# Queries and keys of the last 1024 tokens: seven quadrant products instead of eight

## The chip, the cores and the metric

The kernel runs on one core of a Trainium2 chip. The core's engines work in parallel, each through its own instruction list in order: PE multiplies matrices, ACT, DVE and POOL work on tiles element by element, SP (like the others) issues transfers. Engines wait for each other through semaphores. The metric is the time of one execution in microseconds (us); less is better.

## The reference

One layer of a decoder trunk on 2048 tokens of width 1024, all in float32. Only its first product matters here:

```
hn = _rmsnorm(h, ln_mix[i])
z = hn @ w_in[i]                       # (2048, 1024) @ (1024, 2048)
q = z[..., :512] * (HEAD_DIM ** -0.5)
k = z[..., 512:1024]
v = z[..., 1024:1536]
u = z[..., 1536:]
att = _dilated_attention(q, k, v, slopes)
pool = _multiscale_pool(u, pool_w[i], pool_scale[i])
h = h + concatenate([att, pool]) @ w_out[i]
```

`_multiscale_pool` takes trailing means of u over 2, 4, 8 and 16 tokens (one window for each group of 128 channels), subtracts the token, and multiplies by a 128x128 matrix for each group. A gated MLP, a gate on per-layer embeddings and a last norm follow; the change does not touch them.

## The kernel before, in words

A float32 product is done as three matmuls (`mm3`, L88): each operand is split into a rounded high part (a cast on ACT) and the low rest (a subtraction on DVE or POOL; `split`, L83), and high times high, high times low and low times high are added in PSUM.

`phase_project` (L170) computes z from chunks of tokens that go through it one after the other: chunk 0 (tokens 0 to 255), chunk 1 (256 to 511), chunks 2, 3 and 4 (512 tokens each). Each chunk has four groups of 512 output channels: 0 = q, 1 = k, 2 = v, 3 = u. The list in `order` gives 0, 1, 2, 3, and 0, 1, 3, 2 for chunk 4. A group sums over eight blocks of 128 inputs. One block is one **step**: four tiles by three matmuls of 128x512. A group so has eight steps, and fills four of the eight banks of PSUM; six banks go round in turn among the groups, one ("st") takes the sums of squares and the spread norm, one ("py") the small product of the pooling.

The split weights of q, k and v stay resident from chunk 0. Those of u are loaded in each chunk: `ahead` (L270) issues the loads and, three steps before the use, the ACT cast `wh` and the POOL low `wl`; there are three buffers of each.

The order in which each engine gets its instructions is the order in which the code calls them, and the engines keep to it (`manual_schedule`). Work beside the matmuls is spread by hand:

- After each step `tk.tick()` runs what `tk.later(n, ...)` put off by n steps.
- Step by step in group k, `square` puts the next chunk's squares into `acc` (ACT square, DVE add; one buffer `sq`). In group v `scale` and `spread_` make the norm: small PE products, POOL's power `pw`, four DVE instructions and two PE products into bank "st". In group u `norm_a` multiplies the next chunk's tokens by the norm on DVE, `norm_b` casts the high part (ACT) and subtracts for the low part (DVE).
- A finished group is taken from its banks: q and k by ACT and DVE and stored by SP, v into `vt`, whose stores go out on SP, and for chunk 4 on POOL's queue.
- `pool_branch` (L410) takes u from PSUM on ACT, and for each of its four channel groups later sums the windows on DVE (`ws`; 1, 2, 3 and 4 additions), subtracts the token, splits (ACT `dh`, DVE `dl`), multiplies into "py" (PE), and takes that out (ACT `mh`, DVE `ml`, two stores on POOL's queue). `ml` in `ACFG` says how many steps after the group each starts: 1, 3, 5, 11, and 1, 3, 5, 7 for chunk 4. This work falls into the next chunk's q and k groups, and for chunk 4 into its v group.

Of the kernel before, what the change touches and what calls it, by code (L numbers as in the profile page):

```python
# [168 lines left out]

def phase_project(tc, g, xT, w_in, pool_w, rcnt):  # L170
# [4 lines left out]
    with ExitStack() as ctx:  # L175
        wres = ctx.enter_context(tc.tile_pool(name="a_w", bufs=1, reuse_waits="tile"))
        sb = ctx.enter_context(tc.tile_pool(name="a_sb", bufs=1, reuse_waits="tile"))
        psum = ctx.enter_context(tc.tile_pool(name="a_ps", bufs=6, space=PSUM, reuse_waits="tile"))
# [24 lines left out]
        def load_w(pool, raw, grp, k, tag, bufs, low=None):  # L203
            hi = pool.tile([P, 512], F32R, tag=tag + "h", bufs=bufs, name=f"wh{grp}_{k}")
# [37 lines left out]
        def norm_a(st, k):  # L242
            xk = st.xs[k][:, : st.n]
            nc.vector.tensor_tensor(xk, xk, st.inv[:, : st.n], op=ALU.mult)

        def norm_b(st, k):
            hi = sb.tile([P, CH], F32R, tag="hnh", bufs=KD, name=f"hnh{k}")
            lo = sb.tile([P, CH], F32R, tag="hnl", bufs=KD, name=f"hnl{k}")
            n = st.n
            st.hn.append((hi[:, :n], lo[:, :n]))  # L250
            gain = g.vec[:, V_MIX + k : V_MIX + k + 1]
            nc.scalar.activation(hi[:, :n], st.xs[k][:, :n], AF.Copy, scale=gain)  # L252
            st.low = lambda: nc.vector.scalar_tensor_tensor(  # L253
                lo[:, :n], st.xs[k][:, :n], gain, fp(hi[:, :n]), op0=ALU.mult, op1=ALU.subtract
            )
# [15 lines left out]
        def ahead(i):  # L271
            while done[0] < len(wants) and wants[done[0]][0] <= i:
                w, c, grp, k = wants[done[0]]
                done[0] += 1
                fetch_to(w)
                low = ACFG["low"][min(c, 2)][grp][k % 2]
                low = nc.vector if low else nc.gpsimd
                raw = raws.pop((c, grp, k))
                if grp < 3:
                    held[grp, k] = load_w(wres, raw, grp, k, f"w{grp}", KD, low)  # L280
                else:
                    held[grp, k] = load_w(sb, raw, grp, k, "wu", 3, low)
            fetch_to(i + ACFG["ld"] if i < 8 * 3 - ACFG["ld"] - ACFG["la"] - 1 else i + ACFG["lu"])

# [6 lines left out]
        step = 0  # L291
        for c, (t0, n) in enumerate(chunks):
            cs = slice(t0, t0 + n)
            final = c == len(chunks) - 1
            nxt = None
            for gi, grp in enumerate((0, 1, 2, 3) if not final else (0, 1, 3, 2)):
                if gi == 2 and not final:
# [3 lines left out]
                ps = [psum.tile([P, CH], F32, tag="b1", name=f"z{c}_{grp}_{j}") for j in range(nt)]  # L301
                apart = final and grp == 2
                for k in range(KD if not apart else 0):
# [3 lines left out]
                    ahead(step + ACFG["la"])  # L307
                    step += 1
# [9 lines left out]
                    if gi == 0 and k == 6 and not final:  # L318
# [3 lines left out]
                    if gi == 3 and not final:  # L322
# [15 lines left out]
                    if gi == 0 and c > 0 and k < 2:  # L338
# [57 lines left out]
            cur = nxt  # L396
# [13 lines left out]
def pool_branch(nc, g, sb, psum, c, q, ps, t0, n, tail, rc, pw_h, pw_l, zpair, final):  # L410
# [57 lines left out]
    g.ticker.later(ACFG["ml"][1 if final else 0][q], means)  # L468
# [1432 lines left out]
def tile_layer(ctx, tc, xT, pT, vec, w_in, pool_w, w_out, w_up, w_down, w_gate, w_ple, near_b, far_b, rcnt, outT, upto=9):  # L1901
# [39 lines left out]
    g.dd = [{p: dr.tile([P, CH], F32, tag=f"dd{q}{p}", name=f"dd{q}{p}") for p in ("t1", "t2", "t3", "t4")} for q in range(NF // 2)]  # L1941
    g.h1 = per(KD, [P, S], F32, "h1")
# [85 lines left out]
```

## Time and profile before

| | us |
|---|---|
| median of 3 runs (lowest, highest) | 2395.49 (2394.4, 2397.76) |
| the profiled execution's own time | 2395.75 |
| its span in the profile | 2394.0 |
| PE busy in the span | 2320.2 (97%) |
| DVE, ACT, POOL busy | 1714.3, 1123.5, 571.1 |
| share of PE in the chain that ended last | 78% |

"Busy" is the time an engine spends in instructions. A row of a timeline reads: start (us from the span's start), busy us, engine, line, operation, out<-in by the program's names, shape, and in brackets the idle time ahead of it with the instruction that ended it. A row with x3 is three neighbouring instructions of one kind. A row by groups reads: busy us in all, mean ns of one | idle us ahead of them, and what ended it. `PEclk` is the clock that PE was granted, 1.00 being full speed; over the span its mean is 0.987. In the trace, chunk 2's u group and the start of chunk 3 lie around 194 to 240 us, and the last v group of `phase_project` at about 398 us.

### The profile page before, as it was taken

To read this page: it belongs to the slowest core of one execution; us is meant where nothing else is said; L and a number is where in the kernel's file an instruction comes from. 1 tells how busy PE (TensorE), PEld (TensorE's weight loads), DVE (VectorE), ACT (ScalarE), POOL (GpSimd) and SP (SyncE) were. 2 spreads that over 40 slices of the span, in tenths; PEclk is the share of its full clock that TensorE was granted. 3 is DMA by queue.
4 is the path that set the end of the run, shared out by engine and by line. 5 is a ranking of instruction groups with operands and counts; after the bars stand their busy time and mean duration, and the time that the engine had idled before them with its cause. 6 is when DMAs were issued, how large, how long until landed. Compare 5 with 4: busy or idle time off the path is not lost.

```text
span 2394.0 us, 32736 instructions
## 1 busy us (share of the span) xinstructions
PE 2320.2 (97%) x11251; PEld 1962.7 (82%) x11251; DVE 1714.3 (72%) x2684; ACT 1123.5 (47%) x2040; POOL 571.1 (24%) x552
## 2 busy tenths in 40 slices
PE   8999999999989989999999999999999999999998
PEld 7888887988868868888887787888878888888888
DVE  6645445888864668999999998777766565755665
ACT  5332234988832245454447353544444444444332
POOL 3322122356620133344430664000020000001000
PEclk9999999999999999999999999999999999999999
DMA  7534436877576664556567787444487776754332
GB/s 232 185 132 164 179 130 248 269 239 241 161 262 216 214 203 144 189 189 207 189 212 246 265 277 248 156 147 146 141 317 254 240 243 204 224 172 154 119 102 93
DMA packets 240550, 475.99 MB, mean 199 GB/s; under 512 B 37472, under 2 KB 63904, under 8 KB 237312
## 3 DMA queue, kind: packets, MB, share of 16 engines
q1 hardware_dynamic: 205040, 394.64, 50.2%
q0 software_dynamic: 15696, 51.49, 6.0%
q10 hardware_dynamic: 19648, 27.77, 3.3%
q8 instruction: 88, 1.44, 0.3%
q14 instruction: 78, 0.64, 0.1%
HBM read 309.14 MB, written 156.79 MB: 195 GB/s over the span
## 4 chain that ended last, share of the span: by engine, by line
PE 78%; DVE 8%; DMA 5%; issue 3%; ACT 1%; POOL 0%; SPq 0%; ACTq 0%; DVEq 0%; POOLq 0%
PE ua L1375 16%; PE uc L1375 8%; PE dn L89 5%; PE dn L90 5%; PE dn L91 5%; PE ub L1375 4%; PE z L91 4%; PE z L89 4%; PE z L90 4%; PE o L91 2%; PE o L89 2%; PE o L90 2%; PE tp L604 2%; PE gp L89 2%; PE gp L91 2%
## 5 line engine op out<-in xcount | busy, mean ns | idle before, releaser
L90 PE MATMUL dn<-al,wu 128*128 128x512 f32 x616 | 240.3, 390 | 3.2 <-DVE al L85 3.2
L89 PE MATMUL dn<-ah,wu 128*128 128x512 f32 x616 | 240.1, 390 | 0.0
L91 PE MATMUL dn<-ah,wu 128*128 128x512 f32 x616 | 239.8, 389 | 0.0
L85 DVE TENSOR_TENSOR al<-ra,ah 128x512 fp32r<-128x512 f32 x154 | 105.9, 690 | 110.0 <-ACT ah L84 107.8
L89 PE MATMUL z<-hnh,wh 128*128 128x512 f32 (+1 forms) x480 | 170.5, 355 | 10.8 <-ACT hnh L252 6.3
L90 PE MATMUL z<-hnl,wh 128*128 128x512 f32 (+1 forms) x480 | 170.3, 355 | 2.3 <-DVE hnl L253 2.0
L91 PE MATMUL z<-hnh,wl 128*128 128x512 f32 (+1 forms) x480 | 170.1, 354 | 2.3 <-POOL wl L85 1.7
L84 ACT CAST ah<-ra 128x512 fp32r<-128x512 f32 x154 | 95.2, 620 | 143.8 <-PE dn L91 124.9
L90 PEld LDWEIGHTS dn<-al,wu 128*128 128x128 f32 x616 | 115.6, 188 | 29.1 <-DVE al L85 5.2
L85 DVE TENSOR_TENSOR wu<-ru,wu 128x1024 fp32r<-128x1024 f32 x88 | 134.7, 1530 | 3.9 <-ACT wu L84 3.9
L89 PEld LDWEIGHTS dn<-ah,wu 128*128 128x128 f32 x616 | 115.6, 188 | 24.3 <-ACT ah L84 0.4
L91 PEld LDWEIGHTS dn<-ah,wu 128*128 128x128 f32 x616 | 115.6, 188 | 24.1
L1375 PE MATMUL ua<-s1h,wu 128*128 128x512 f32 x352 | 116.8, 393 | 4.4 <-ACT ug L1602 4.4
L1375 PE MATMUL ua<-s4h,wu 128*128 128x512 f32 x352 | 117.2, 394 | 2.6 <-ACT uv L1623 2.6
L1375 PE MATMUL uc<-a22h,wu 128*128 128x512 f32 x352 | 116.9, 393 | 2.7 <-DVE uv L1398 2.7
L1375 PE MATMUL ub<-a12h,wu 128*128 128x512 f32 x352 | 115.7, 389 | 1.1 <-ACT a12h L1431 1.1
L1375 PE MATMUL ua<-s2h,wu 128*128 128x512 f32 x352 | 115.8, 390 | 0.8 <-ACT ug L1576 0.7
L1375 PE MATMUL uc<-s3h,wu 128*128 128x512 f32 x352 | 115.7, 389 | 0.0
L1375 PE MATMUL ua<-a11h,wu 128*128 128x512 f32 x352 | 115.5, 389 | 0.0
L155 DVE TENSOR_TENSOR acc<-acc,sq 128x512 f32<-128x512 f32 (+1 forms) x125 | 81.3, 650 | 47.3 <-ACT sq L154 33.8
L85 DVE TENSOR_TENSOR wu<-rw,wu 128x512 fp32r<-128x512 f32 x149 | 101.1, 688 | 18.7 <-ACT wu L84 18.4
L89 PEld LDWEIGHTS z<-hnh,wh 128*128 128x128 f32 x480 | 94.5, 197 | 22.7 <-ACT hnh L252 6.3
(335 smaller groups left out, 6664.8 us busy)
## 6 DMA issues: line engine op xcount, KB each, us to landing
ru<-in_w_up_dram SPq DMA_DIRECT2D x66, 512.0 KB, 4.2
wr<-in_w_in_dram SPq DMA_DIRECT2D x64, 256.0 KB, 4.4
rw<-in_w_down_dram SPq DMA_DIRECT2D x61, 256.0 KB, 3.7
nt<-h SPq DMA_DIRECT2D x56, 256.0 KB, 3.9
td<-t SPq DMA_DIRECT2D x22, 512.0 KB, 2.6
t<-td SPq DMA_DIRECT2D x22, 512.0 KB, 3.7
nt<-in_w_down_dram POOLq DMA_DIRECT2D x44, 256.0 KB, 5.4
ra<-oq0s SPq DMA_DIRECT2D x44, 256.0 KB, 4.1
```

The costliest lines, as they stand in the source:

```text
L84: nc.scalar.copy(hi, src)
L85: (low or nc.gpsimd).tensor_tensor(lo, src, fp(hi), op=ALU.subtract)
L89: nc.tensor.matmul(ps, wh, ah, start=first, stop=False, skip_group_check=again)
L90: nc.tensor.matmul(ps, wh, al, start=False, stop=False, skip_group_check=again)
L91: nc.tensor.matmul(ps, wl, ah, start=False, stop=last, skip_group_check=again)
L155: nc.vector.tensor_tensor(acc[:, :n], acc[:, :n], sq[:, :n], op=ALU.add)
L604: nc.tensor.transpose(st.tp[:, bs], st.ee[:, bs], g.ident)
L1375: nc.tensor.matmul(pst, x[:, ksl], y, start=first and k == 0 and n == 0, stop=k == HK - 1 and n == 2, skip_group_check=True)
```

## The change

Queries and keys of chunks 3 and 4 are no longer computed in their own groups. With the normed tokens as a 2 by 2 block matrix (chunk by half of the inputs) and the weights as another (half of the inputs by q or k), the block product takes seven products of blocks, four steps each, instead of eight: 28 steps, in `pair`. In the code a11, a12 = the two halves of chunk 3's inputs, a21, a22 = those of chunk 4; b11, b21 = the two halves of q's weights, b12, b22 = those of k's. What else this brings:

- `GROUPS` reorders: chunk 2 does k, q, v, u; chunks 3 and 4 do u and v alone. So the u groups of chunks 2 and 3 follow each other, then comes chunk 3's v, then the 28 steps of `pair`, then chunk 4's u and v. Chunk 4's tokens are loaded, squared (in chunk 3's u group) and normed (from chunk 3's v group on) earlier, and chunk 3's tokens lie in other buffers ("y"), which half of k's weights used.
- `quad_sums`: for each of four blocks q, four loads on SP (step 1), four POOL subtractions that give t1, t3, t2, t4 (L354) and four stores to DRAM on POOL's queue (L355), one pair a step, over 40 steps from chunk 2's second group on. In `pair` the 16 sums come back as weights: load, ACT cast `whx`, POOL low `wlx`.
- In `pair`: for 16 steps an operand is split (ACT `ah`, DVE `al`); sums of tokens on DVE (`sum_2`) and POOL (L446, L455). Products 0, 2 and 3 of the seven are copied out of their banks on ACT (`kept`), later ones are added to the copies on DVE (`whole`) and then split and stored as q or k.
- Banks: `pair` sums in four of the six, A, and in a second set of four, B: the two left over, "st" and "py".
- Gain and norm are multiplied in one DVE instruction for chunks 3 and 4 (`st.scaled`); chunk 4's norm is copied from PSUM by ACT.
- The pooling of chunks 2 to 4 starts 1, 3, 5, 7 steps after its group.

```diff
+QUADS = (
+    ("a11", "b11", True, True),
+    ("a12", "b21", False, True),
+    ("s2", "t2", True, False),
+    ("s3", "t3", False, True),
+    ("s1", "t1", True, False),
+    ("a22", "t4", False, False),
+    ("s4", "b22", True, False),
+)
...
+        GROUPS = ((0, 1, 2, 3), (0, 1, 2, 3), (1, 0, 2, 3), (3, 2), (3, 2))
...
+        def quad_sums(q):
...
+            def subtract(n):
+                b11, b12, b21, b22 = b
+                o, x, y = ((b11, b12, b11), (b12, b22, b12), (b22, b22, b11), (b21, b21, b22))[n]
+                nc.gpsimd.tensor_tensor(o, x, y, op=ALU.subtract)
+                nc.gpsimd.dma_start(g.qd[q][("t1", "t3", "t2", "t4")[n]], o)
...
+            return [load, None, None] + [lambda n=n: subtract(n) for n in range(4)] + [None, None, None]
...
+        def pair(old, new):
+            A = [ring("za") for _ in range(4)]
...
+            for m in range(28):
+                x, q = divmod(m, HK)
+                pa, wb, chain, starts = QUADS[x]
+                ahead(step[0] + ACFG["la"])
...
+                if x == 1 and q == 0:
+                    tk.flush()
+                if not chain and starts and q == 0:
+                    B = [psum.tile([P, CH], F32, tag=f"p{n}", name="zb") for n in spare]
+                    B += [psum1.tile([P, CH], F32, tag=t, name="zb") for t in ("st", "py")]
+                bank = A if chain else B
...
+                for j in range(4):
+                    js = slice(j * P, (j + 1) * P)
+                    mm3(nc, bank[j], wh[:, js], wl[:, js], ah, al, starts and q == 0, q == HK - 1, not starts)
+                tk.tick()
...
+                if m < HK:
+                    normed_(HK + m)
+                    nc.gpsimd.tensor_tensor(a22[m], a21[m], a22[m], op=ALU.add)
+                if 1 <= m <= HK:
+                    sum_2(m - 1)
+                if 1 <= m < HK:
+                    operand(m + 7)
+                if 8 <= m < 17 or 21 <= m < 25:
+                    operand(m + 3)
+                if HK <= m < 2 * HK:
+                    normed_(m - HK)
+                    nc.gpsimd.tensor_tensor(a21[m - HK], a11[m - HK], a21[m - HK], op=ALU.subtract)
...
+            if final:
+                pair(old, cur)
...
+                    if c > 1 and (c, gi) > (2, 0) and sums:
+                        (sums.pop(0) or (lambda: None))()
...
-                    if gi == 1 and not final:
+                    if gi == (0 if last else 1) and not final:
                         square(nxt, k)
...
-    g.ticker.later(ACFG["ml"][1 if final else 0][q], means)
+    g.ticker.later(ACFG["ml"][1 if t0 >= CH else 0][q], means)
```

Three places show how the engines' lists change. The rows are line, operation, out<-in with a running number behind each name.

The first is POOL after chunk 2's u group. Before, POOL has nothing there but the halo copies of the pooling and its stores (`tail` is the last 15 tokens, `mh4` and `ml4` are the stored parts):

```order
L85 TENSOR_TENSOR wl3_7_2462<-wr3_7_2421,wh3_7_2461 128x512
L419 COPY u_2533<-tail0_438 128x15
L422 COPY tail0_438<-u_2533 128x15
L419 COPY u_2537<-tail1_439 128x15
L422 COPY tail1_439<-u_2537 128x15
L419 COPY u_2541<-tail2_440 128x15
L422 COPY tail2_440<-u_2541 128x15
L419 COPY u_2545<-tail3_441 128x15
L422 COPY tail3_441<-u_2545 128x15
L463 DMA mh4_103<-mh_2613 128x512
```

Now, with chunk 3's u group behind it (`wl3_2` to `wl3_5` are that group's weights, b and `qd2` the quadrant sums), the piece after the halo copies reads:

```order
L627 COPY tail3_457<-u_2624 128x15
L85 TENSOR_TENSOR wl3_3_2633<-wr3_3_2568,wh3_3_2632 128x512
L354 TENSOR_TENSOR b_2518<-b_2522,b_2518 128x512
L355 DMA qd2t3_413<-b_2518 128x512
L85 TENSOR_TENSOR wl3_4_2664<-wr3_4_2591,wh3_4_2663 128x512
L354 TENSOR_TENSOR b_2522<-b_2522,b_2516 128x512
L355 DMA qd2t2_412<-b_2522 128x512
L85 TENSOR_TENSOR wl3_5_2689<-wr3_5_2636,wh3_5_2688 128x512
L354 TENSOR_TENSOR b_2520<-b_2520,b_2522 128x512
L355 DMA qd2t4_414<-b_2520 128x512
L85 TENSOR_TENSOR wl3_6_2726<-wr3_6_2667,wh3_6_2725 128x512
L668 DMA mh4_103<-mh_2720 128x512
```

The lows of chunk 3's u weights and the quadrant sums moved into the stretch in which chunk 2's pooling runs.

DVE in the same stretch, from the start of chunk 2's pooling. Before:

```order
L430 TENSOR_TENSOR ws_2565<-u_2533 128x526
L441 SCALAR_TENSOR_TENSOR ws_2565<-ws_2565,u_2533 128x512
L253 SCALAR_TENSOR_TENSOR hnl6_2531<-x3_1_2001,vec_79,hnh6_2530 128x512
L446 TENSOR_TENSOR dl_2569<-ws_2565,dh_2568 128x512
L253 SCALAR_TENSOR_TENSOR hnl7_2573<-x3_1_2001,vec_79,hnh7_2572 128x512
L430 TENSOR_TENSOR ws_2601<-u_2537 128x526
L430 TENSOR_TENSOR ws_2603<-ws_2601 128x524
L441 SCALAR_TENSOR_TENSOR ws_2603<-ws_2603,u_2537 128x512
L446 TENSOR_TENSOR dl_2607<-ws_2603,dh_2606 128x512
L462 SCALAR_TENSOR_TENSOR ml_2614<-py_2609,vec_79,mh_2613 128x512
```

Now:

```order
L635 TENSOR_TENSOR ws_2652<-u_2612 128x526
L646 SCALAR_TENSOR_TENSOR ws_2652<-ws_2652,u_2612 128x512
L291 TENSOR_TENSOR hnl6_2610<-x3_1_2011,hnh6_2609 128x512
L651 TENSOR_TENSOR dl_2656<-ws_2652,dh_2655 128x512
L155 TENSOR_TENSOR acc_2436<-acc_2436,sq_2684 128x512
L291 TENSOR_TENSOR hnl7_2661<-x3_1_2011,hnh7_2660 128x512
L635 TENSOR_TENSOR ws_2708<-u_2616 128x526
L635 TENSOR_TENSOR ws_2710<-ws_2708 128x524
L646 SCALAR_TENSOR_TENSOR ws_2710<-ws_2710,u_2616 128x512
L155 TENSOR_TENSOR acc_2436<-acc_2436,sq_2722 128x512
L651 TENSOR_TENSOR dl_2714<-ws_2710,dh_2713 128x512
L667 SCALAR_TENSOR_TENSOR ml_2721<-py_2716,vec_79,mh_2720 128x512
```

Chunk 4's sums of squares (`acc`) stand between the pooling's instructions, and ahead of `ml`.

The third place is ACT around the second block product of `pair`. Before, in chunk 4's q group, it has the pooling of chunk 3 and the evictions of q:

```order
L443 CAST dh_3350<-ws_3347 128x512
L461 ACTIVATE mh_3357<-py_3353,vec_79 128x512
L461 ACTIVATE mh_3392<-py_3388,vec_79 128x512
L368 ACTIVATE qh_3410<-z4_0_0_3248 128x512
L368 ACTIVATE qh_3416<-z4_0_1_3249 128x512
L368 ACTIVATE qh_3422<-z4_0_2_3250 128x512
L368 ACTIVATE qh_3428<-z4_0_3_3251 128x512
```

Now, from the third operand of `pair` (`ah` of t, the sum that `sum_2` makes on DVE) over the copies `r` of the first block product (`za`) to the fourth operand:

```order
L84 CAST ah_3236<-t_3233 128x512
L396 COPY r_3240<-za_3119 128x512
L396 COPY r_3240<-za_3120 128x512
L396 COPY r_3241<-za_3121 128x512
L396 COPY r_3241<-za_3122 128x512
L290 CAST hnh0_3265<-x4_0_2437 128x512
L290 CAST hnh1_3282<-x4_0_2437 128x512
L290 CAST hnh2_3301<-x4_0_2437 128x512
L290 CAST hnh3_3320<-x4_0_2437 128x512
L84 CAST whx_11_3325<-wr_3287 128x512
L364 ACTIVATE qh_3344<-r_3240 128x512
L84 CAST ah_3350<-t_3262 128x512
```

The copies that free the banks A stand behind three operands' casts, and the fourth operand's cast behind the first q eviction.

More of the change, by code (lines that the diff above doesn't have):

```diff
@@ L203, in load_w @@
         def load_w(pool, raw, grp, k, tag, bufs, low=None):
+            if grp == 1 and k < HK:
+                if k == 0:
+                    early.extend(wres.tile([P, HK, CH], F32R, tag="y", bufs=2, name=f"y{x}") for x in "hl")
+                hi, lo = (y[:, k, :] for y in early)
+                split(nc, hi, lo, raw, low)
+                return hi, lo
             hi = pool.tile([P, 512], F32R, tag=tag + "h", bufs=bufs, name=f"wh{grp}_{k}")
@@ L243, in norm_a @@
             xk = st.xs[k][:, : st.n]
-            nc.vector.tensor_tensor(xk, xk, st.inv[:, : st.n], op=ALU.mult)
+            if st.scaled:
+                gain = g.vec[:, V_MIX + k : V_MIX + k + 1]
+                nc.vector.scalar_tensor_tensor(xk, xk, gain, st.inv[:, : st.n], op0=ALU.mult, op1=ALU.mult)
+            else:
+                nc.vector.tensor_tensor(xk, xk, st.inv[:, : st.n], op=ALU.mult)
         def norm_b(st, k):
@@ L249, in norm_b @@
             n = st.n
-            st.hn.append((hi[:, :n], lo[:, :n]))
+            st.hn[k] = hi[:, :n], lo[:, :n]
+            if st.scaled:
+                nc.scalar.copy(hi, st.xs[k])
+                st.low = lambda: nc.vector.tensor_tensor(lo, st.xs[k], fp(hi), op=ALU.subtract)
+                return
             gain = g.vec[:, V_MIX + k : V_MIX + k + 1]
@@ L255, in norm_b @@
             )
-        order = [(c, gi, grp, k) for c in range(len(chunks))
-                 for gi, grp in enumerate((0, 1, 2, 3) if c < len(chunks) - 1 else (0, 1, 3, 2)) for k in range(KD)]
-        wants = [(i, c, grp, k) for i, (c, gi, grp, k) in enumerate(order) if c == 0 or grp == 3]
+        order = []
+        for c, grps in enumerate(GROUPS):
+            if c == 4:
+                order += [(c, "x", m) for m in range(28)]
+            order += [(c, grp, k) for grp in grps for k in range(KD)]
+        wants = []
+        for i, (c, grp, k) in enumerate(order):
+            if grp == "x" and QUADS[k // HK][1][0] == "t":
+                wants.append((i - 4 if k < 11 else i, c, grp, k))
+            elif c == 0 or grp == 3:
+                wants.append((i, c, grp, k))
         raws, fetched = {}, [0]
@@ new lines, in phase_project, with emit_q, emit_k @@
+        for q in range(HK):
+            sums += quad_sums(q)
+        def emit_q(row, j, src):
+            hi, lo = zpair("q", CH)
+            nc.scalar.activation(hi, src, AF.Copy, scale=QSCALE)
+            nc.vector.scalar_tensor_tensor(lo, src, QSCALE, fp(hi), op0=ALU.mult, op1=ALU.subtract)
+            cs = slice(row * CH, (row + 1) * CH)
+            rdma(nc, g.qh[j][:, cs], hi)
+            rdma(nc, g.ql[j][:, cs], lo)
+        def emit_k(row, j, src):
+            hi, lo = (by_residue(z) for z in zpair("k", CH))
+            pr = src.rearrange("p (j r) -> p r j", r=4)
+            nc.scalar.copy(hi, pr)
+            nc.vector.tensor_tensor(lo, pr, fp(hi), op=ALU.subtract)
+            rdma(nc, residues(g.kk[j][:, 0], row * CH, CH), hi)
+            rdma(nc, residues(g.kk[j][:, 1], row * CH, CH), lo)
@@ L285, in phase_project, with half_inv @@
+        def half_inv(st):
+            spread_(st)
+            inv = sb.tile([P, CH], F32, tag="acc", name="inv")
+            nc.scalar.copy(inv, st.inv)
+            st.inv = inv
         cur = first = loads(0)
@@ L294, in phase_project @@
             final = c == len(chunks) - 1
-            nxt = None
-            for gi, grp in enumerate((0, 1, 2, 3) if not final else (0, 1, 3, 2)):
-                if gi == 2 and not final:
+            last = c == 3
+            if final:
+                pair(old, cur)
+            nxt = last_ if last else None
+            for gi, grp in enumerate(GROUPS[c]):
+                if last and gi == 1:
+                    tk.later(2, lambda st=nxt: scale(st))
+                    tk.later(4, lambda st=nxt: half_inv(st))
+                if gi == 2:
                     tk.later(2, lambda st=nxt: scale(st))
@@ L300, in phase_project @@
                 nt = 4 if grp != 2 else n // P
[L301 removed]
+                ps = [ring(f"z{c}_{grp}_{j}") for j in range(nt)]
                 apart = final and grp == 2
```

114 lines of the change are left out of this document (101 added, 13 removed).

## The prediction

> **What bounds the kernel now.** I read the page's span and busy rows first, then the chain that ended last, then the waits of PE and a table of stages of `phase_project`, last the timelines of single engines.
>
> ```profile
> span 2394.0 us, 32736 instructions
> PE 2320.2 (97%) x11251; PEld 1962.7 (82%) x11251; DVE 1714.3 (72%) x2684; ACT 1123.5 (47%) x2040; POOL 571.1 (24%) x552
> ...
> PE 78%; DVE 8%; DMA 5%; issue 3%; ACT 1%; POOL 0%; SPq 0%; ACTq 0%; DVEq 0%; POOLq 0%
> ```
>
> PE is the bound, so a matmul removed is worth its time as long as PE goes on without waits. From 150 us to 400 us, where chunks 2 to 4 are, it waits once, for 0.4 us. The stages from chunk 2's u group on, by window (PE, weight loads, DVE, ACT, POOL busy, granted clock, DMA share, GB/s):
>
> ```profile
> PE py L89 <- DVE ml L462: 0.4, 1, 0.4
> ...
> 194.00:216.00 22.00, 22.00 (x99) 18.23 (x98) 13.14 (x18) 9.60 (x16) 8.52 (x9) 1.00 0.79 289
> 216.00:239.00 23.00, 23.00 (x103) 19.03 (x103) 11.78 (x18) 6.23 (x10) 4.83 (x11) 1.00 0.30 109
> ```
>
> The first row is a u group (token norms on DVE, lows of weights on POOL), the second the q group behind it with the pooling. PE is full in both; DVE has half of its time left, and heavy DVE work and heavy POOL work are in different windows. The change puts both into one.
>
> **What is removed.** The casts of weights follow PE's steps:
>
> ```profile
> 358.09 0.62 ACT L84 CAST wh<-wr 128x512 fp32r<-128x512 f32 x1 [2.10 <-PE z L90]
> 360.81 0.62 ACT L84 CAST wh<-wr 128x512 fp32r<-128x512 f32 x1 [2.10 <-PE z L90]
> ```
>
> A step lasts 360.81 - 358.09 = 2.72 us. 28 steps instead of 32 save 4 x 2.72 = 10.9 us.
>
> **The price of DVE beside POOL.** The lows and sums that are added stand in one queue each, and the trace shows what the two queues do to each other:
>
> ```profile
> 47.73 4.08 DVE L85 TENSOR_TENSOR wl<-wr,wh 128x512 fp32r<-128x512 f32 x3
> ...
> 48.10 3.16 POOL L85 TENSOR_TENSOR wl<-wr,wh 128x512 fp32r<-128x512 f32 x2 [1.37 <-ACT wh L84]
> ...
> 100.43 3.75 POOL L85 TENSOR_TENSOR wl<-wr,wh 128x512 fp32r<-128x512 f32 x3
> ...
> L446 DVE TENSOR_TENSOR dl<-ws,dh 128x512 fp32r<-128x512 f32 x12 | 8.3, 692 | 8.0 <-ACT dh L443 8.0
> ...
> 208.61 1.26 DVE L253 SCALAR_TENSOR_TENSOR hnl<-x,vec,hnh 128x512 fp32r<-128x512 f32 x1 [3.90 <-ACT hnh L252]
> ...
> 213.36 0.74 DVE L253 SCALAR_TENSOR_TENSOR hnl<-x,vec,hnh 128x512 fp32r<-128x512 f32 x1
> 214.02 0.68 DVE L244 TENSOR_TENSOR x<-x,bc 128x512 f32<-128x512 f32 x1
> ...
> 209.79 0.68 DVE L244 TENSOR_TENSOR x<-x,bc 128x512 f32<-128x512 f32 x1
> ...
> 217.19 0.20 POOL L419 COPY u<-tail 128x15 f32<-128x15 f32 x1
> ...
> L463 POOL DMA_DIRECT2D mh<-mh x12 | 6.7, 559 | 79.5 <-ACT mh L461 74.1 <-ACT qh L368 5.3
> ```
>
> Alone, DVE takes 0.69 us for a subtraction (`dl`) and POOL 3.75 / 3 = 1.25 us. Together, three on DVE take 4.08 us: 4.08 - 3 x 0.69 = 2.0 us more, for two of POOL's. `hnl` takes 1.26 us beside POOL's lows (they run from 208.0 us) and 0.74 us without; `x`, which reads one input from PSUM, keeps its 0.68 us beside them. So a POOL instruction that meets a row of two-input DVE work costs DVE a price p of about 1.1 us, between 0 (they miss each other) and 1.25 us (all of it). I take 1.1, the nearer row being one of back-to-back queues, as they will stand here. DVE instructions otherwise start 214.02 - 213.36 = 0.66 us apart. POOL's last two rows give 0.2 us for a halo copy and 0.56 for issuing a store.
>
> **What is added, in order of time.** PE is in order, so each wait adds to the end. Times below count from the start of chunk 3's u group.
>
> *Chunk 3's u group.* POOL first does the low of the third weight (cast at 0 to 0.6, then 1.25), a quadrant subtraction (1.25), its store's issue (0.55) and a halo copy (0.2): 3.85 us, and the first window sum on DVE waits for it. Up to `ml` of the first pooling group, which frees bank "py" for the second, DVE has 11 instructions (11 x 0.66 = 7.3; two are the added squares' sums), POOL seven tensor instructions beside them (four lows, three subtractions: 7 x 1.1 = 7.7), ACT's cast and square are waited for (1.2), `ml` takes 0.75: 20.8 in all. PE wants "py" after five steps, a small product and a 0.2 us bank wait: 5 x 2.72 + 0.68 + 0.2 = 14.5. Wait: 6.3 us, or 7p - 1.4. For the next, DVE needs seven instructions, one of POOL's, ACT's cast and scaled copy (0.62 + 0.69) and `ml`: 20.8 + 4.6 + 1.1 + 1.3 + 0.75 = 28.6; PE wants it at 20.8 + 0.68 + 2 x 2.72 = 26.9. Wait: 1.7 us.
>
> *Start of chunk 3's v,* at 28.6 + 0.68 + 2.72 = 32.0. Its third bank waits for the copy of u on ACT:
>
> ```profile
> 214.17 1.54 ACT L420 COPY u<-z 128x512 f32<-128x512 f32 x3
> 216.39 0.59 ACT L420 COPY u<-z 128x512 f32<-128x512 f32 x1 [0.68 <-DVE ws L441]
> ...
> 224.19 0.69 ACT L461 ACTIVATE mh<-py,vec 128x512 fp32r<-128x512 f32 x1 [2.54 <-PE py L91]
> ...
> L155 DVE TENSOR_TENSOR acc<-acc,sq 128x512 f32<-128x512 f32 x14 | 9.7, 691 | 7.4 <-ACT sq L154 7.3
> L154 ACT ACTIVATE sq<-x 128x512 f32<-128x512 f32 x14 | 8.8, 629 | 6.2 <-DVE acc L155 6.2
> L84 ACT CAST wh<-wr 128x512 fp32r<-128x512 f32 x24 | 14.3, 618 | 22.4 <-PE z L90 9.5 <-DMA wr<-in_w_in_dram 4.5 <-PE z L91 4.3
> ```
>
> Today ACT starts these copies about 2 us ahead of the group's end. Now the fourth pooling group's cast stands ahead of them, which waits for six DVE instructions after 28.6 (32.6), then a square, a scaled copy and another square: 32.6 + 0.62 + 0.63 + 0.69 + 0.63 + 0.59 = 35.8. The third bank is wanted at 32.0 + 1.36 = 33.4. Wait: 2.4 us (0 if DVE has caught up).
>
> *Chunk 3's v.* After two steps and the sums of squares over tokens, at 41.3, come POOL's power (1.5 with ACT's part), two short and two long DVE instructions, then `ml` and `dl` (2 x 0.17 + 4 x 0.65 = 2.9): 45.7, where PE wants `dl` a step after 41.3, at 44.0: 1.7 us; the next small product is 0.3 late: 2.0 us. If POOL is busy beside it, the short ones are not short:
>
> ```profile
> 46.77 0.17 DVE L118 CAST ph<-pw 128x2 fp32r<-128x2 f32 x1 [0.67 <-POOL pw L110]
> 46.97 0.16 DVE L119 TENSOR_TENSOR pl<-pw,ph 128x2 f32<-128x2 f32 x1
> ...
> 99.41 1.04 POOL L110 TENSOR_TENSOR pw<-ms,mhalf 128x4 f32<-128x4 f32 x1 [5.37 <-ACT ms L108]
> ...
> 269.23 1.27 DVE L118 CAST ph<-pw 128x4 fp32r<-128x4 f32 x1 [5.50 <-POOL pw L110]
> ```
>
> *Start of `pair`,* at 45.7 + 5 steps + 3.0 for small products = 62.3. Banks three and four are v's, and are freed by DVE's lows of v, behind three pooling groups and six norms in one queue: 25 instructions, three POOL subtractions and 1.9 of hand-offs, 45.7 + 16.5 + 3.3 + 1.9 = 67.4, wanted 62.3 + 1.36 = 63.6. Wait: 3.8 us.
>
> *Step 8 of `pair`.* It needs A, whose copies stand on ACT behind the cast of the third summed operand. DVE gets to that sum with 17 instructions and seven of POOL's, then cast and first copy: 67.4 + 11.2 + 7.7 + 0.6 + 0.6 = 87.5; and the queue loses 4.3 us, as today, to the fourth cast of v, which waits for the first v tile's stores:
>
> ```profile
> 284.14 0.53 SPq L391 DMA_DIRECT2D vn<-vt  x1
> ...
> 288.43 0.59 ACT L388 CAST vt<-z 128x512 fp32r<-128x512 f32 x1 [3.69 <-DMA vf<-vt]
> ```
>
> That is 288.43 - 284.14; so 91.8, and PE wants it at 63.6 - 1.36 + 3.8 + 8 x 2.72 + 0.68 = 88.5. Wait: 3.3 us (0 if the v stores no longer hold it).
>
> *Step 11.* After the other copies (93.6) and a cast (94.2) DVE makes four lows beside four POOL sums (4 x 1.76 = 7.0), then the first q sum, its ACT eviction, the operand's cast and its low (2.7): 104.0; wanted 91.8 + 3 x 2.72 = 100.0. Wait: 4.0 us. *Step 12* wants its last bank at 108.7, DVE frees it at 104.0 + 7 x 0.66 + 1.1 = 109.7: 1.0 us. From there to step 27 a step has two or three DVE instructions and a POOL low (2 + 1.1 us in 2.72), and I charge nothing.
>
> At nothing, too: the 32 added loads on SP and 16 stores (DMA share is 0.30 to 0.79 in the windows above; if the cover went, a weight would come late at step 11 first), the q and k stores of chunk 3, which come later but with all of chunk 4's u and v before their use, and the joined gain and norm, one instruction for one.
>
> Sum: 0.2 + 6.3 + 1.7 + 2.4 + 2.0 + 3.8 + 3.3 + 4.0 + 1.0 = 24.7 us of waits, less 10.9: +13.8 us. On the profiled execution's own 2395.75 us (span 2394.0, 1.75 around it; the median of the runs, 2395.49, is 0.3 below) this is 2409.6, say 2410 us.
>
> **A rule against a row.** POOL's stores may hold DVE as well:
>
> ```profile
> 1355.62 2.27 DVE L1474 TENSOR_TENSOR x<-yg 128x512 f32<-128x512 f32 x1
> ...
> 1355.44 0.56 POOL L1511 DMA_DIRECT2D dd2t<-nt  x1 [0.30 <-POOL nt L1510]
> 1356.03 1.31 POOL L1510 TENSOR_TENSOR nt<-nt 128x512 f32<-128x512 f32 x1
> ```
>
> The DVE instruction spans the store's issue and the subtraction behind it, 0.56 + 1.31, and its own time. With seven stores beside DVE's queue that is 7 x 0.55 = 3.9 us more, 2414; I leave it out of the sum, since one row cannot part it from the subtraction alone, and keep it in the range. The Trainium skill, "SBUF — State Buffer", section "Who interferes with whom", says that a tensor_tensor with two SBUF inputs contends with a GpSimd (POOL) instruction's reads, and infers that it does not hold off descriptor generation; by it these 3.9 us are 0. The 4.08 us row agrees with its first half.
>
> **Rivals.** *Hidden (faster):* POOL's instructions fall into DVE's gaps in chunk 3's u group. The first wait is gone at p = 0.2 (7p = 1.4), and what follows comes earlier by as much: with p at 0 the first `ml` is done at 20.8 - 7.7 = 13.1, the queues stay ahead, and all 10.9 us stay: 2385. For it: from 194 to 216 us DVE and POOL together have 21.7 of 22 us and PE never waits; against: `hnl` at 1.26 in that very window.
>
> *Partly hidden (same):* engines catch up between stages, and only the load counts. From chunk 3's u group to step 11 DVE has 91 instructions, 91 x 0.66 = 60 us, meets 24 of POOL's, 26 us, and waits 5 us for ACT: 91 us against 80 of PE's, a wait of 11: 2396, between 2391 and 2400.
>
> *The clock falls (slower still).* After PE waits it gets a lower clock:
>
> ```profile
> 65.29 0.39 PE L89 MATMUL z<-hnh,wh 128*128 128x256 f32 x1 [2.40 <-ACT wh L84]
> ...
> 66.00:70.00 4.00, 3.36 (x15) 3.36 (x16) 4.00 (x9) 2.09 (x5) 2.05 (x3) 0.58 0.36 112
> 70.00:74.00 4.00, 4.00 (x35) 4.00 (x35) 3.53 (x12) 2.17 (x6) 1.06 (x7) 1.00 0.41 79
> ```
>
> After a 2.40 us wait a 4 us window has 0.58, so 0.42 x 4 = 1.7 us are lost. Five of my waits are 2.4 us or longer: 5 x 1.7 = 8.5, 2418. Against: some waits will be split over several matmuls, and then nothing is lost. The Trainium skill, "TensorE: Matmul & The Clock Gate", Part 1, puts half rate after an idle window of about 3.4 us; by it three of the waits would count (6.3, 3.8, 4.0), an estimate of 5.1 us and 2415; the row has it after 2.40.
>
> **How the numbers follow.** Chances: waits as summed 0.54, with the clock 0.10, partly hidden 0.17, hidden 0.19. The sum's own range, with p from 0.6 to 1.25 (the first wait 2.8 to 7.4) and the waits on ACT and stores between nothing and twice, is about 2401 to 2418. The range, 2388 to 2424, leaves out the fully hidden case and a tail above. A change of 0.2%, 4.8 us, is about what a measurement of this kernel can tell: faster 0.19, same 0.17, slower 0.64.
>
> **What would show it.** Right: PE waits between 216 and 325 us for "py" behind `ml`, for `vt`, `r` and `al`, DVE subtractions of 1.3 to 1.8 us there, 2.72 us a step again late in `pair`. A first `ml` on time proves the price wrong; waits that add to 11 us, the partly hidden case; windows of 0.6 clock, the last rival. A wait of some us for weights from DRAM would be a cause I charged nothing.

## The result and the profile after

The changed kernel is slower: 2414.9 us (median of 5 runs, 2409.79 to 2420.91) against 2395.49 (5 runs, 2389.87 to 2397.76), a ratio of 1.0087 with a 95% interval of 1.0063 to 1.011. By the ratio that is 15 to 26 us. The profiled execution took 2418.72 us. Its page begins, span, engines and the share of the chain that ended last:

```profile
span 2416.9 us, 32882 instructions
...
PE 2323.8 (96%) x11203; PEld 1960.2 (81%) x11203; DVE 1759.3 (73%) x2720; ACT 1146.8 (47%) x2085; POOL 636.9 (26%) x608
...
PE 74%; DVE 10%; DMA 5%; issue 4%; ACT 2%; POOL 1%; SPq 0%; ACTq 0%; DVEq 0%; POOLq 0%
```

PE has 48 matmuls less (11203 for 11251), which is the four steps saved, and is yet busy 3.6 us longer: at a lower clock the matmuls follow each other more slowly (0.43 us apart from 244.33 us on, where the granted clock is 0.5; 0.23 us ahead of the wait there). What PE waited for between 216 and 400 us, where before there was one wait of 0.4 us (what was waited for, us in all, times, longest):

```profile
PE py L89 <- DVE ml L667: 9.8, 3, 8.1
PE za L89 <- DVE vt L594: 4.3, 1, 4.3
PE z L89 <- DVE kl L374: 3.6, 2, 2.3
PE za L90 <- DVE al L85: 2.0, 1, 2.0
PE z L89 <- ACT u L625: 1.3, 2, 1.1
```

That is 21.0 us. The clock behind four of them, by windows (the columns as in the prediction, the granted clock being third from the end):

```profile
241.00:245.00 4.00, 2.12 (x5) 1.73 (x6) 3.97 (x5) 0.88 (x2) 3.02 (x4) 0.50 0.56 154
245.00:249.00 4.00, 4.00 (x12) 3.10 (x12) 2.71 (x4) 1.73 (x3) 0.18 (x1) 0.61 0.39 113
...
289.00:293.00 4.00, 1.97 (x5) 1.59 (x6) 3.17 (x6) 0.20 (x1) 0.54 (x1) 0.51 0.54 219
293.00:297.00 4.00, 4.00 (x13) 3.15 (x12) 1.05 (x2) 1.67 (x4) 0.00 (x0) 0.63 1.02 414
...
325.00:330.00 5.00, 4.82 (x14) 3.87 (x15) 3.60 (x7) 3.31 (x6) 2.64 (x2) 0.67 0.63 221
...
380.00:384.00 4.00, 3.98 (x9) 3.18 (x10) 0.00 (x0) 0.62 (x1) 1.27 (x1) 0.50 0.65 245
```

Summed over windows of 2 us from 200 to 440 us, PE's busy time by the missing share of the clock is 11.2 us; in the profile of before it is 1.6. The clock so costs 9.6 us.

The last rows needed are the first matmul of the attention behind the projection, before and after:

```profile
400.07 0.28 PE L573 MATMUL sn<-ks,qhh 128*128 128x256 f32 x1
...
427.69 0.28 PE L778 MATMUL sn<-ks,qhh 128*128 128x256 f32 x1
```

It is 27.6 us later. As a second mark I take PE's matmul number 1040 of the trace (counted from 0), in chunk 2's u group, at 198.8 us before and 203.3 after: called "start of chunk 2's u" in the expectations. From mark to attention, **the stretch**, it is 201.2 us before and 224.4 after, +23.2: 10.9 saved, 21.0 of waits, 9.6 of clock; the 3.5 us that are left I put down to the edges of the nine waits, where matmuls stand wider apart. The other 4.5 us lie ahead of the change's stages, and the 4.7 us between 27.6 and the difference of the spans, 22.9, came back in the later stages. Their length scatters: from 1986 to 2000 us over the 14 profiles of this document, 1994 and 1992 in the two of the kernel before.

### The profile page after: what moved, and what is told of

Its sections match the earlier page's. It is cut to its first block, busy times and chain, and to the rows that moved or that the text cites. A ratio compares the mean times of both kernels' runs of the same rounds, so it can differ in the third digit from the quotient of the medians.

```text
span 2416.9 us, 32882 instructions
## 1 busy us (share of the span) xinstructions
PE 2323.8 (96%) x11203; PEld 1960.2 (81%) x11203; DVE 1759.3 (73%) x2720; ACT 1146.8 (47%) x2085; POOL 636.9 (26%) x608
## 4 chain that ended last, share of the span: by engine, by line
PE 74%; DVE 10%; DMA 5%; issue 4%; ACT 2%; POOL 1%; SPq 0%; ACTq 0%; DVEq 0%; POOLq 0%
PE ua L1580 16%; PE uc L1580 8%; PE dn L90 5%; PE dn L91 5%; PE dn L89 5%; PE ub L1580 4%; PE o L91 2%; PE o L89 2%; PE o L90 2%; PE tp L809 2%; PE z L89 2%; PE z L90 2%; PE z L91 2%; PE gp L89 2%; PE gp L91 2%
## 5 line engine op out<-in xcount | busy, mean ns | idle before, releaser
L89 PE MATMUL z<-hnh,wh 128*128 128x256 f32 (+1 forms) x304 | 108.3, 356 | 14.6 <-ACT hnh L294 6.1
L90 PE MATMUL z<-hnl,wh 128*128 128x256 f32 (+1 forms) x304 | 108.0, 355 | 2.6 <-DVE hnl L295 2.4
L91 PE MATMUL z<-hnh,wl 128*128 128x256 f32 (+1 forms) x304 | 108.0, 355 | 2.3 <-POOL wl L85 1.7
L877 POOL TENSOR_TENSOR s<-s,ev 64x512 f32<-64x512 f32 x60 | 76.7, 1287 | 122.9 <-DMA s<-ev 118.5
```

Source lines behind the costliest of these rows:

```text
L89: nc.tensor.matmul(ps, wh, ah, start=first, stop=False, skip_group_check=again)
L90: nc.tensor.matmul(ps, wh, al, start=False, stop=False, skip_group_check=again)
L91: nc.tensor.matmul(ps, wl, ah, start=False, stop=last, skip_group_check=again)
L877: sums.later(3, lambda: nc.gpsimd.tensor_tensor(dst[mine], dst[mine], t[mine], op=ALU.add))
```

## The experiments

Each ratio is to the kernel before, run on the same chip; the stretch of each kernel is from its one profile. One relief alone changes the whole time by little more than the intervals tell, so the waits and the stretch are read first. In the runs the kernel before had medians of 2390.7 to 2394.2.

### Store issues on SP (stores_on_sp)

```diff
-                nc.gpsimd.dma_start(g.qd[q][("t1", "t3", "t2", "t4")[n]], o)
+                nc.sync.dma_start(g.qd[q][("t1", "t3", "t2", "t4")[n]], o)
```

> The changed kernel with the 16 stores of quadrant sums issued by SP instead of POOL. If issuing a store on POOL holds DVE as its subtractions do, the two DVE instructions of 3.5 us in chunk 3's u group shrink to about 1.8 each, the first PE wait for bank py falls from 8.1 us to 4 to 5, and with the clock loss behind it the time falls by 4 to 7 us against the changed kernel (2414.9). If only POOL's tensor instructions hold DVE, that wait stays over 6.5 us and the time within 2 us.

The first wait for py fell to 5.9 us, between the two forecasts (4 to 5, and over 6.5), the stretch to 221.8; the time, ratio 1.0103 [1.0084, 1.0123], did not fall. DVE and POOL in chunk 3's u group, first in the changed kernel, then in this one:

```profile
230.21 3.51 DVE L291 TENSOR_TENSOR hnl<-x,hnh 128x512 fp32r<-128x512 f32 x1
233.64 3.47 DVE L635 TENSOR_TENSOR ws<-u 128x526 f32<-128x526 f32 x1
237.15 0.70 DVE L635 TENSOR_TENSOR ws<-ws 128x524 f32<-128x524 f32 x1
...
230.03 0.56 POOL L355 DMA_DIRECT2D qd2t<-b  x1 [0.30 <-POOL b L354]
230.62 1.30 POOL L85 TENSOR_TENSOR wl<-wr,wh 128x512 fp32r<-128x512 f32 x1
231.87 1.29 POOL L354 TENSOR_TENSOR b<-b 128x512 f32<-128x512 f32 x1
...
236.83 0.56 POOL L355 DMA_DIRECT2D qd2t<-b  x1 [0.30 <-POOL b L354]
```

```profile
227.63 1.78 DVE L291 TENSOR_TENSOR hnl<-x,hnh 128x512 fp32r<-128x512 f32 x1
229.33 1.79 DVE L635 TENSOR_TENSOR ws<-u 128x526 f32<-128x526 f32 x1
...
227.09 1.76 POOL L85 TENSOR_TENSOR wl<-wr,wh 128x512 fp32r<-128x512 f32 x1
228.82 1.73 POOL L354 TENSOR_TENSOR b<-b 128x512 f32<-128x512 f32 x1
```

Without these stores in POOL's queue the two engines take turns, one instruction each, 1.1 us dearer for DVE than alone (1.78 for 0.68): the price of the prediction. With the stores, a DVE instruction that began during a store's issue waited for that and for both of POOL's instructions behind it: 3.51 us, and 3.47 for the next. The issue alone held nothing: the instruction at 237.15 us began in the middle of one, with no POOL tensor instruction behind it, and took its 0.70 us. So what the stores cost DVE is its turn: POOL's next two instructions went ahead. That the time as a whole did not fall with the 2.6 us of the stretch is within what the runs scatter.

### Without the subtractions (no_subtraction)

The 16 subtractions are left out, the weights are stored as loaded; the products of q and k are other ones, their number and the stores are the same.

```diff
-                nc.gpsimd.tensor_tensor(o, x, y, op=ALU.subtract)
                 nc.gpsimd.dma_start(g.qd[q][("t1", "t3", "t2", "t4")[n]], o)
```

> The changed kernel without the 16 POOL subtractions of weight quadrants (the unsubtracted weights are stored in their place, the 16 stores stay on POOL). By the price of DVE beside POOL (about 1.1 us for each), three subtractions less ahead of the first ml: the wait of 8.1 us for py falls to 4 to 5 and the time by 4 to 7 us. If the store issues are what holds DVE, the wait stays over 6.5 us.

```profile
PE py L89 <- DVE ml L666: 5.1, 3, 2.6
PE z L89 <- DVE kl L373: 4.2, 2, 2.3
PE za L89 <- DVE vt L593: 2.6, 1, 2.6
PE za L90 <- DVE al L85: 2.3, 1, 2.3
PE z L89 <- ACT u L624: 2.3, 2, 2.1
PE za L89 <- ACT r L395: 1.6, 1, 1.6
```

The longest wait for py is 2.6 us, less than the 4 to 5 forecast; the wait at pair's start falls with it, from 4.3 to 2.6. But a wait for u grows to 2.1 and one for r, which was not there, takes 1.6: a queue that is late in one place hides that it is late in the next. Ratio 1.0071 [1.0053, 1.009], stretch 218.3.

### Sums early (sums_early)

```diff
-                    if c > 1 and (c, gi) > (2, 0) and sums:
+                    if (c, gi) >= (1, 2) and sums:
```

> The changed kernel with the quadrant sums begun in chunk 1's v group, so that the last subtraction stands in chunk 2's v group, and chunk 3's u and v groups have no POOL work but lows and pooling. By the theory that POOL's work beside the pooling is the main wait: py wait 8.1 us to under 1.5, time down by 8 to 13 us to about 2404. By the rival that DVE's own load (pooling and chunk 4's squares in one group) is enough to be late: a wait of 4 us or more stays, time down by under 6.

The waits for py fell to 2.9 us in all (longest 2.0), the stretch to 215.0, 9.4 us less. The longest wait lies between the two forecasts (under 1.5, and 4 or more), nearer to the theory's. The time did not fall (1.0096 [1.008, 1.0112]): the added work stands in chunk 1 now, and PE's mark in chunk 2 comes at 207.4 for 203.3, behind a 5.8 us wait for u's weights. A relief that moves work has to find a place that is free.

### k's copies by residues (k_sorted)

`r` of the fourth product is copied and added in the order of residues, so that the cast and the low read neighbours:

```diff
-                nc.scalar.copy(rs[x][j], src)
+                if x == 3:
+                    nc.scalar.copy(by_residue(rs[x][j]), src.rearrange("p (j r) -> p r j", r=4))
+                else:
+                    nc.scalar.copy(rs[x][j], src)
...
-            pr = src.rearrange("p (j r) -> p r j", r=4)
+            pr = by_residue(src) if sorted_ else src.rearrange("p (j r) -> p r j", r=4)
```

> The changed kernel with the fourth product's copies laid out in the order of residues that the stores of k want, so that the cast and the low of k for chunk 4 read neighbouring elements of SBUF (before: 1.1 us each, every fourth element). By the theory that these 1.1 us make the chain of add, cast, operand cast, low longer than a step and that this causes PE's 2.3 and 1.35 us waits for kl behind pair: cast and low take about 0.65 us, the two waits fall to under 1 us together, the clock loss there too, time down by 3 to 6 us. Rival: the chain is as long from its hand-offs; waits and time stay.

The cast in the changed kernel, from SBUF and (last) from PSUM, and here:

```profile
361.05 1.09 ACT L373 CAST kh<-x 128x512 fp32r<-128x512 f32 x1 [1.82 <-DVE x L400]
...
375.88 0.58 ACT L373 CAST kh<-za 128x512 fp32r<-128x512 f32 x1 [0.49 <-DMA qh<-qh]
```

```profile
358.29 0.62 ACT L373 CAST kh<-x 128x512 fp32r<-128x512 f32 x1 [1.44 <-DVE x L405]
```

1.09 us becomes 0.62; the waits behind pair go from 2.30 and 1.35 to one of 1.9, where under 1 was forecast. So the strided read was one part, and a chain of additions and evictions ahead of it the other. The Trainium skill, "SBUF — State Buffer", section "Door 1: The DMA port swizzle", tells of lines of 16 bytes, and of a price for each access that goes to a new one; every fourth float is one for each line, and the 1.09 against 0.62 us agrees. Reading every fourth float from PSUM took 0.58. Stretch 220.8, ratio 1.0086 [1.0069, 1.0103], not resolved.

### Sums on DVE (sums_on_dve)

This is the sharpest test of the price: work is given to the engine that is late.

```diff
-                nc.gpsimd.tensor_tensor(o, x, y, op=ALU.subtract)
+                nc.vector.tensor_tensor(o, x, y, op=ALU.subtract)
...
-                    nc.gpsimd.tensor_tensor(a22[m], a21[m], a22[m], op=ALU.add)
+                    nc.vector.tensor_tensor(a22[m], a21[m], a22[m], op=ALU.add)
...
-                    nc.gpsimd.tensor_tensor(a21[m - HK], a11[m - HK], a21[m - HK], op=ALU.subtract)
+                    nc.vector.tensor_tensor(a21[m - HK], a11[m - HK], a21[m - HK], op=ALU.subtract)
```

> The changed kernel with the 16 quadrant subtractions and the 8 sums of tokens in pair moved from POOL to DVE, the engine that is late. By the price (a POOL tensor instruction costs DVE about 1.1 us, while the same instruction on DVE takes 0.69) this gives DVE time back: the first wait for py falls from 8.1 us by 3 x 0.4 and by what back-to-back POOL instructions after a store cost (about 2), to 4.5 to 6, the wait of 2.0 us for al goes under 1, time down by 3 to 7 us against the changed kernel. By the rival that DVE is simply overloaded by its own instructions, adding 24 instructions to it makes it later: first wait over 9 us, time up by 3 to 10 us.

```profile
PE py L89 <- DVE ml L667: 4.3, 2, 3.4
PE z L89 <- DVE kl L374: 3.7, 2, 2.2
PE za L89 <- DVE vt L594: 3.2, 1, 3.2
PE z L89 <- ACT u L625: 2.3, 2, 2.1
PE zb L89 <- DVE r L400: 0.9, 1, 0.9
PE za L90 <- DVE al L85: 0.3, 1, 0.3
```

With 24 instructions more, DVE is earlier: the first wait falls from 8.1 to 3.4 us (4.5 to 6 forecast) and that for al from 2.0 to 0.3. Over the stretch DVE has 185 instructions for 168, and is busy 138.1 us for 140.8; the stretch is 216.1, 8.3 us less. The rival, that DVE is overloaded by its own work alone, falls. The time's ratio, 1.0088 [1.0073, 1.0103], shows none of it; its interval and that of the changed kernel leave room for most of the 8.3 us, and what the later stages did in the unprofiled runs is not known.

### All reliefs together (relieved, relieved_more, adds_first)

Kernel relieved: quadrant sums in chunk 2's k, q and v groups, chunk 4's squares in chunk 2's v group, k by residues, pair's sums on DVE; chunk 4's tokens are loaded earlier for it.

```diff
-                    if c > 1 and (c, gi) > (2, 0) and sums:
+                    if c == 2 and gi < 3 and sums:
...
-                    if gi == (0 if last else 1) and not final:
+                    if gi == 1 and c < 3:
                         square(nxt, k)
+                    if c == 2 and gi == 2 and k > 3:
+                        square(last_, 2 * k - 8)
+                        square(last_, 2 * k - 7)
```

> All reliefs at once, with the seven products kept: quadrant sums in chunk 2's k, q and v groups (six steps a block, still on POOL), chunk 4's squares in chunk 2's v group, k's copies laid out by residues, pair's sums of tokens on DVE. By the theory (waits come from DVE and POOL work that meets in chunk 3's u group and in pair): waits for py, u and al under 3 us in all in place of 13, the wait at pair's start 2 to 3 us, the one behind pair 2; time 2392 to 2400, between the kernel before and 0.3% over it. If the waits only move to chunk 2, the time stays over 2405.

Ratio 1.0016 [1.0005, 1.0026], median 2396.24: of the 0.87% all but 0.16% is gone, and the median lies in the forecast's 2392 to 2400. 9.4 us of waits are left from 216 to 400 us, the stretch is 203.6.

Kernel relieved_more adds the lows of u's weights from chunk 2 on and of pair's on DVE (`low` in `ACFG` and the call of `load_w`) and starts the pooling at steps 0, 2, 4, 6.

> As the kernel before it, and the lows of u's weights from chunk 2 on and of the quadrant sums in pair on DVE as well, so that POOL has no tensor instructions in these stages but the quadrant sums, and the pooling of chunks 2 and 3 starts one step earlier. By the price another 0.4 us for each low comes back to DVE and the wait at pair's start falls under 1.5: 2388 to 2396. By the rival that DVE is then overloaded (8 lows of 0.69 us a group more): py waits of 2 us and more, time over 2400.

Ratio 1.0013 [0.9999, 1.0027], median 2395.13 (2388 to 2396 forecast), stretch 202.6; the wait at pair's start is gone, one of 2.2 for r and one of 1.1 for u came in.

Kernel adds_first then puts the additions that free banks ahead of all evictions, and chunk 2's lows back on POOL:

```diff
+                    if x in (1, 4, 5):
+                        of = {1: 0, 4: 3, 5: 2}[x]
+                        for j in range(4):
+                            tk.later(1, lambda j=j, of=of, src=bank[j]: add(j, of, src))
```

> The last kernel with two edits: in pair the four additions that free a product's banks stand together ahead of the evictions that follow them, and the lows of chunk 2's u weights are back on POOL. By the theory the waits of 2.2 us for r at step 12 and 1.6 us for kl behind pair fall to under 1 us together, and the 1.1 us for u at the start of chunk 3's u goes: PE waits from 200 to 400 us under 3.5 us in all (7.0 in the last kernel), time 2386 to 2392, at or below the kernel before. Rival: the waits are those of the chain of casts on ACT, stay within 1 us of 7, and the time stays at 2393 to 2398.

The waits here from 190 us on, and the window of the stretch in the changed kernel and (second) here:

```profile
PE za L90 <- DVE al L85: 1.3, 1, 1.3
PE py L89 <- DVE ml L685: 1.3, 3, 0.6
PE py L90 <- DVE dl L669: 0.8, 1, 0.8
PE z L89 <- DVE vt L608: 0.6, 1, 0.6
PE z L91 <- POOL wl L85: 0.6, 1, 0.6
PE za L89 <- ACT ah L84: 0.4, 1, 0.4
PE z L89 <- ACT u L643: 0.2, 1, 0.2
```

```profile
203.33:427.69 224.36, 202.62 (x839) 161.89 (x838) 140.80 (x168) 84.66 (x149) 101.19 (x112) 0.94 0.49 175
...
201.03:398.29 197.26, 192.51 (x840) 156.00 (x839) 133.26 (x202) 79.51 (x143) 29.64 (x54) 1.00 0.52 185
```

PE's matmuls are the same in both. POOL's busy time falls from 101.2 to 29.6 us, its instructions being DVE's now or in chunk 2, and DVE, with 202 instructions instead of 168, is busy 7.5 us less. The clock is full. The two waits it was made for, for r and kl, are gone; from 200 us on 4.6 us are left, where under 3.5 was forecast. Stretch 197.3, 3.9 us under the kernel before; ratio 1.0001 [0.9989, 1.0012], so no faster than before. The forecast of 2386 to 2392 was just missed (2393.17).

### The loads ahead of the change (before_again, loads_in_place, reworked, loads_on_act)

The marks in chunk 2 are 0 to 9 us later than before in the changed kernel and its variants. SP's order is planned, not written, and the loads of `quad_sums` stand early in it. SP in the changed kernel in chunk 0 (b are the weights to be subtracted, wr those of u):

```profile
48.73 3.17 SPq L223 DMA_DIRECT2D wr<-in_w_in_dram  x3
51.95 0.90 SPq L348 DMA_DIRECT2D b<-in_w_in_dram  x2
53.99 0.33 SPq L223 DMA_DIRECT2D wr<-in_w_in_dram  x1
54.36 0.91 SPq L348 DMA_DIRECT2D b<-in_w_in_dram  x2
...
62.62 0.90 SPq L348 DMA_DIRECT2D b<-in_w_in_dram  x2
```

> The kernel before, once more with a profile, to see what differs between two executions ahead of the change's stages. In the profile at hand PE starts chunk 2's u group 2.4 to 4.6 us earlier than in all changed kernels. If that is the change's doing, it does so again; if it is the waits for the first weights of u (2.4 us in that profile, 3.2 to 4.9 in the others), this one may lie anywhere in 0 to 4 us later.

The mark of the kernel before came again at 198.8 us, its wait for the first u weight at 2.6 (2.4 in the first profile; 3.2 to 4.9 in the changed kernel and the eight variants above). So the longer wait is not chance. The lateness of the mark is another matter: no_subtraction has the same loads, and its mark is at 199.0 us. Ahead of the mark PE's waits add up to 17.8 us before and 18.3 in the changed kernel, and the clock lost there, summed as above, to 6.1 and 11.2 us. Most of the 4.5 us of that profile is lost clock, not waiting for loads.

```diff
-                        nc.sync.dma_start(t, w_in[k * P : (k + 1) * P, x * CH : (x + 1) * CH])
+                        nc.scalar.dma_start(t, w_in[k * P : (k + 1) * P, x * CH : (x + 1) * CH])
```

> The changed kernel with the 16 loads of the quadrant sums' weights issued from ACT's queue at their place in the code, instead of SP's, whose order is planned: there the first six (1.5 MB) are issued from 50 to 63 us, among the loads of chunk 0's u weights. By the theory that these make the u weights late: PE's wait for the first u weight goes from 3.4 back to about 2.5 us, chunk 2's u group starts 2 to 4 us earlier (before 198.8, changed 203.3), the waits from 216 us on stay, time down by 2 to 4 us. Rival (the early lateness is chance, or the clock): start of chunk 2's u group stays at 201 to 204.

That wait fell from 3.41 to 2.81, but the mark came at 201.6 for 203.3, in the range of the rival; stretch 225.3, ratio 1.0094 [1.0079, 1.011], no gain to be seen. The loads are one part of the early lateness at most.

The same for adds_first, once with POOL's queue and the first additions a step later (reworked), once with ACT's (loads_on_act):

> The kernel adds_first with the same loads on POOL's queue at their place (they stand beside no pooling of 512 tokens there), and the first additions of pair one step later, behind the operand that step 11 waits for. By the theory: chunk 2's u group starts at 198 to 200 us, PE waits from 200 to 400 us under 4.5 us, and of the 10.9 us saved about 6 to 8 are left: 2386 to 2390, 0.2 to 0.35% faster than the kernel before. If the early lateness stays, 2391 to 2395.

> The kernel reworked with the 16 loads on ACT's queue instead of POOL's, where their issue stood ahead of the subtractions and chunk 2's k and q groups lost 6.7 us. By the theory chunk 2's three groups ahead of u take 53 to 55 us again (60.1 in reworked, 53.3 before), the stages behind keep their 195 us (before 201), and the attention starts at 394 to 397 us in place of 400: 2387 to 2391, about 0.2% faster than the kernel before. If ACT's queue holds its casts up instead, chunk 2 takes over 57 us and the time is 2392 to 2396.

In both the early wait is 1.6 us, and the stretch 194.9 and 195.6, some 6 us under the kernel before. With POOL's queue chunk 2 lost it again (mark at 204.9). With ACT's the attention starts at

```profile
395.53 0.28 PE L796 MATMUL sn<-ks,qhh 128*128 128x256 f32 x1
```

4.5 us ahead of the kernel before, and the profiled execution took 2384.56 us. But the 12 runs have a median of 2392.85 (2384.56 to 2397.5), ratio 1.0003 [0.9989, 1.0016], and reworked 2393.2, 1.0003 [0.9991, 1.0016]. Both forecasts, 2386 to 2390 and 2387 to 2391, were missed. No version beat the kernel before by what a measurement can tell. Whether the unprofiled runs lose the 4.5 us in the later stages, or ahead of them, is open: only one execution of each has a trace. That of loads_on_act was the fastest of its 12 runs, that of reworked, 2401.51 us, the slowest of its 11, with 2000 us in the later stages.

## Why the prediction was right, and where it was not

The direction, the mechanism and most of the places came as forecast; the sum, +13.8, is under the measured 15 to 26, for reasons that partly cancel.

- **The saving** of 10.9 us is there: 48 matmuls less, and PE keeps the pace where nothing is late (2.72 us for the step of pair that begins at 311.83 us).
- **The price of POOL beside DVE** was right for instructions that take turns: 1.1 us each. The first wait, 6.3 us in the forecast, is 5.9 in stores_on_sp and 8.06 in the changed kernel. That it is so near is partly luck. From the start of chunk 3's u group (219.65 us) the first `ml` ends at 23.2 us for the forecast 20.8: DVE waits 3.1 us for ACT's casts and squares, not 1.2, the first window sum starts at 4.35, not 3.85, and what DVE's rows last beyond 0.69 us each adds up to the forecast 7.7, but with the two of 3.5 us in it. In stores_on_sp, without those, it is 6.2, and with the same 3.1 for ACT the 20.8 is met by two errors that cancel.
- **The stores on POOL** make the difference of 2.2 us between the two waits. The prediction named them ("POOL's stores may hold DVE as well", 3.9 us) and left them out of the sum. I read the rule of the Trainium skill, "SBUF — State Buffer", section "Who interferes with whom", as a price of 0; it speaks only of DVE holding off descriptor generation, not of the reverse, and the 2.2 us are about half of the 3.9.
- **The second ml** (1.7 forecast) was on time: after 8 us of PE's wait DVE had caught up. **The third bank of v** 1.1 for 2.4, **the norm in v** 0.86 + 0.91 for 2.0 (both for "py" behind `ml`, where the forecast had `dl` first), **the start of pair** 4.33 for 3.8.
- **Step 8** (3.3) did not wait. The fourth cast of v did come late (at 295.33 us, the third having ended at 289.2), but PE ran at 0.51 and 0.63 of its clock in the same 8 us, and each copy (312.79 to 314.83) was ahead of its bank's matmuls in step 8, which began at 314.55 us. **Step 11** waited 1.98 for 4.0, **step 12** not.
- **From step 12 to 27 "I charge nothing"** was wrong at the end: 2.30 and 1.35 us for kl behind pair. The chain of addition, cast, operand, low for the last q and k tiles is longer than a step, the more so as k's casts read every fourth element (1.09 us, not 0.62).
- **"At nothing, too: the 32 added loads"** was wrong in the other place: not at step 11, but in chunk 0, where SP's order puts six of them among u's first weights. PE's wait for the first of these is 3.41 us for 2.40: 1.0 us that the sum lacks. Most of the mark's 4.5 us is clock lost ahead of it (11.2 us for 6.1), and how much of that the longer wait brought on is open.
- **The clock** stood as a rival of 8.5 us with a chance of 0.10. It cost 9.6, and is no rival but part of the same case: the lower clock came with the waits. It fell after 4.33 and 8.06 us, and after 1.98 and after 2.30 with 1.35; so the row of 2.40 was the better guide than the rule of the Trainium skill, "TensorE: Matmul & The Clock Gate", Part 1, which asks for some 3.4 us of idling. But the row is no rule either: in no_subtraction the clock stayed full after waits of 2.59, 2.64 and 2.35 us.

So the waits, 24.7 forecast and 21.0 measured, were nearly right in all, too high inside pair and missing at its end; the terms that were mis-sized are the clock (0 in the sum, 9.6 measured), the edges of the waits (0, about 3.5) and the early loads (0, about 1).

## What to carry to other kernels

When the bound engine is to do less, look first at what the added work does to the engines that feed it, in the stage where it stands: a POOL instruction that takes turns with DVE's cost DVE more than the same instruction done on DVE itself (1.1 against 0.69 us here), so with a late DVE the work is better done on DVE, or moved to a stage where DVE is idle. Price each wait of PE with the clock that may follow it: the 21 us of waits came with 13 us that PE's matmuls took longer (9.6 and 3.5). And where one queue's order is planned, read that order too: loads with free buffers go as early as they can, into somebody else's rush.

## What the runs showed of the hardware that was not expected

- Two-input DVE instructions that began while POOL issued a store, with POOL tensor instructions directly behind it, waited for the issue and for these: 3.51 and 3.47 us with two, 2.22 with one (no_subtraction, at 233.29 us), against 1.78 in turn without the store. It is not so each time: at 243.35 us in the changed kernel one went ahead in the same place and took 0.69. With nothing behind the issue it took 0.70.
- A wait of PE of about 2 us can be followed by a lower clock, and its length alone does not tell: 0.67 over 5 us after 1.98 us of waiting, but 1.00 after 2.64 us in relieved (at 276 us); after 1.61 us it fell in the changed kernel (at 107 us) and did not in the kernel before (at 105 us).
- In these traces the clock falls to one half, for 3.4 us or two or three times that (in the changed kernel 326.7 to 330.1, 289.1 to 295.9 and 237.9 to 248.1 us), as if it were set anew every 3.4 us. With the 14 traces cut into such pieces from 30 to 440 us, the half clock follows every piece in which PE idled over 0.6 of the time, and no piece at full clock in which it idled under 0.4. So it counts where a wait falls: the 2.64 us in relieved lie half in one piece and half in the next, 0.39 and 0.38 of them.
- A cast on ACT that read every fourth float of SBUF took 1.09 us for 0.62; from PSUM it took 0.58, as a plain one does (0.59, v's at 295.33 us).
